# A decoder trunk layer on one core: the second gate's weight rows moved behind the first experts, a fifth ring slot, x loaded first

## The chip, the cores and the metric

The kernel runs on one core of a Trainium2 chip. The metric is the device time of one execution in microseconds; the time given for the kernel is the median of three executions.

## The reference, cut to what matters

One layer on 256 tokens of width 2048, all in float32. Everything with a weight is a matrix product; the modulation vectors come from one product of a single row.

```
mod = silu(c) @ w_ada + b_ada                 # one row, 2048 x 12288
sh1, sc1, g1, sh2, sc2, g2 = split(mod, 6)
h = rmsnorm(x, norm1_g) * (1 + sc1) + sh1
proj = h @ w_in                               # 2048 x 4928
o_a = HGRN2 recurrence on 4 x 1024 columns of proj, 8 heads
o_b = latent attention (q_a, kv_a, k_pe columns of proj), 8 heads, causal
x = x + g1 * (concat(o_a, o_b) @ w_out)       # 2048 x 2048
h2 = rmsnorm(x, norm2_g) * (1 + sc2) + sh2
y = MoE(h2): top-1 of 4 groups, top-2 of 8 experts in it; 32 SwiGLU experts,
    w_gate, w_up 2048 x 512, w_down 512 x 2048 each
x = x + g2 * y
```

## The kernel before, in words

**The weight ring.** All large weights are read once, as tiles `wch` of 128 x 4096 (2048 KB; some are smaller), by one queue, SP's, in the order of the list `items` (built from L104 on). A tile needs a free slot of the ring: RING = 4 slots at first, two more once the temporaries of the first part are closed (after `wout` 0, 1), and a seventh after the first part has ended. `ring_fill` (L165) issues the next load whenever `ring_done` (L183) frees a slot, so the list sets the order of the transfers and, with the text of the program, that of the work on each engine. A scheduler moves single instructions within that.

**The order of the list.** Two chunks of `ad1` (modulation columns for the first 512 columns of sh1 and sc1), `w_in` in quarters of the contraction (`wh` for halves of the first, `win` after) with twelve `adt` chunks merged in, the up-projections of q and kv, `w_out` in two halves of four chunks, and then 32 experts of four `gu` and two `dn` chunks. The other modulation chunks (`mods`: g1, a mixed block m2, g2 and at2) are set behind the items of `last` and the second half of `w_out` by the numbers in SPREAD.

**Two ways to compute the modulation.** An `ada` chunk holds 256 rows of w_ada by 2048 columns; `ada_chunk` multiplies it on TensorE with the silu(c) column as the stationary operand, L299 in the profile (`pada`, 8 matmuls in the program, 16 rows in the trace), and sums over eight chunks in one PSUM bank. `ada_end` copies the sum to `rows`, transposes it to columns (L312, `pcol`), or adds it to the row `brow` for g2. An `adt` or `at2` chunk holds transposed columns; `adt_chunk` multiplies it on VectorE by silu(c), broadcast over the partitions in `gate`, with a sum along the row: two passes of 128 x 2048 a chunk, L277 in the profile. at2 is the second half of sh2 and sc2.

**Projections.** `dense` (L413) splits each weight tile into a rounded part (ScalarE, L421) and the rest (VectorE, L422), and multiplies three products (L429 to L431 where the weights are stationary, L436 to L438 where the tokens are). Four split buffers lie between these engines. For `w_out`, `end` (L577) adds the gated result to x (L581). `hgrn` and `mla` (the attention) run in two halves between the chunks of `last`; each ends in transposes of its result (`pmt`, L567 and L844), which the output projection multiplies. `ptr` (L524) are the transposes at the head of an HGRN sweep, after a chain on VectorE and ScalarE.

**Routing and experts.** After `w_out` the router's result is computed in a chain of small instructions, and groups of four experts follow. For each, `dispatch` gathers the tokens' columns (L996), L1064 multiplies the `gu` chunks, `hidden` makes the SwiGLU product, `down` (L1037) multiplies the `dn` chunks (L1042), with the second gate multiplied into each piece of the result on VectorE (L1046), and `combine` (L1019) scatters the group's result back. `gate_rows` spreads g2 over the partitions after expert 0's `gu` chunks.

**The start.** `pc` (bias and gain columns), `pos_i`, one w_ada chunk, then x in four tiles, then the ring up to four chunks. `norm1` squares x (two tiles on ScalarE, two on VectorE), sums, takes the reciprocal root and multiplies x by it in eight pieces (L348). `make_h` then applies scale and shift (L391) and splits h.

Of the kernel before, what the change touches and what calls it, by code (L numbers as in the profile page):

```python
# [20 lines left out]
RING, NARENA, NTEMP, NSPLIT, RING2 = 4, 14, (8, 6), 4, 2  # L21

SPREAD = (1, 4, 7, 5, 5, 3, 1, 1, 1, 1, 1, 1, 0)
# [16 lines left out]
P_W = 154  # L40
# [4 lines left out]
def tile_hybrid_layer(ctx, tc, A, out):  # L45
# [44 lines left out]
    pos_i = cpool.tile([P, 2], I32, name="pos_i")  # L90
    nc.sync.dma_start(pc, A["pcol"])
    nc.sync.dma_start(pos_i, A["pos"])
# [14 lines left out]
    mods = [("ada", b, ch) for b in ("g1", "m2", "g2") for ch in range(8)] + [("at2", kt) for kt in range(8, 16)]  # L107
# [24 lines left out]
    items += experts  # L132
    index = {it: i for i, it in enumerate(items)}

    def source(it):
# [9 lines left out]
        if k == "ada":  # L145
            return A["w_ada"][("g1", "m2", "g2").index(it[1]), it[2]], 4096
        if k == "at2":
            return A["w_ada_t2"][it[1] - 8], 4096
# [16 lines left out]
    def ring_fill():  # L165
        while ring["next"] < ring["limit"]:
# [7 lines left out]
            nc.sync.dma_start(t[:, :cols], src)  # L174
# [13 lines left out]

    def log_exp_tables(inst):

        load = S.preload_act_table_set("natural_log_exp_and_others")
        tc.add_manual_dep(load.ins, inst.ins.name, mybir.DependencyInfo(mybir.DependencyClass.NoSync, mybir.DependencyReason.DATA),
                          reason="tables")
# [15 lines left out]
    crow = tmp([1, 1024], "crow"), tmp([1, 1024], "crow")  # L209
    for h in range(2):  # L210
        nc.scalar.dma_start(crow[h], A["crow"][:, 1024 * h:1024 * h + 1024])
# [5 lines left out]
    brow = big([P, 512], "brow")  # L217
    nc.scalar.dma_start(brow[0:128:32], A["b_g"])
# [10 lines left out]
    one_row = cpool.tile([1, P], F32, name="one_row")  # L229
    V.memset(one_row, 1.0)  # L230
    for h in range(4):
        ps = pm("pc")
        PE.matmul(ps, one_row, crow[h // 2][:, 512 * (h % 2):512 * (h % 2) + 512], start=True, stop=True)
        g = gate[:, 512 * h:512 * h + 512]
        i = S.activation(g, ps, AF.Sigmoid)
        if h == 3:
            log_exp_tables(i)
        V.tensor_mul(g, g, ps)

    acc = {}  # L240
    rows = cpool.tile([P, 512], F32, name="rows")
    sh1 = cpool.tile([P, 16], F32, name="sh1")
# [26 lines left out]
    def adt_chunk(it, sh, a, b, gain):  # L269

        w = ring_get(it)
        i = it[1]
# [31 lines left out]
    def ada_end(b):  # L304
        if b == "g2":
            for j in range(4):
                V.tensor_add(brow[32 * j:32 * j + 1], brow[32 * j:32 * j + 1], acc[b][32 * j:32 * j + 1])
            return
# [6 lines left out]
        if b == "g1":  # L315
            mod_shift(g1, t, P_BA + 64, 16)
        else:
            mod_shift(sh2[:, 0:8], t[:, 0:8], P_BA + 32, 8)
            mod_scale(a2[:, 0:8], t[:, 8:16], P_BA + 48, P_N2, 8)

    def norm1():

        sq = [big([P, 1024], "sq") for _ in range(4)]
        flat = [x.rearrange("p a b -> p (a b)") for x in xx]
        for j in range(4):
            if j < 2:
                S.activation(sq[j], flat[j], AF.Square)
            else:
                V.tensor_mul(sq[j], flat[j], flat[j])
        V.tensor_add(sq[0], sq[0], sq[1])  # L330
        V.tensor_add(sq[2], sq[2], sq[3])
        V.tensor_add(sq[0], sq[0], sq[2])
        V.tensor_add(sq[1][:, :512], sq[0][:, :512], sq[0][:, 512:])
        ps = pm("pss")
        for i in range(2):
            PE.matmul(ps[:, :256], ones, sq[1][:, 256 * i:256 * i + 256], start=i == 0, stop=i == 1)
# [894 lines left out]
```

## Time and profile before

| | us |
|---|---|
| median of three executions | 1521.19 (1522.1, 1519.09, 1521.19) |
| profiled execution | 1516.6 |
| its span, from the first instruction to the last | 1514.8 |
| TensorE busy | 1116.8 (74% of the span) |
| VectorE busy | 627.1 (41%) |
| ScalarE busy | 335.9 (22%) |
| read from HBM | 570.88 MB, 378 GB/s over the span |

The span lacks 1.8 us of the execution's time, which lie around it. TensorE's clock has two levels, 1.2 and 2.4 GHz; the profile gives the granted clock of a stretch as a share of the higher one, and it was 0.881 on the mean here. A stage of the program is a stretch of the span with the same kind of chunks; the bounds used below are 34.3 (first projection matmul), 232 (last pass of `w_in`'s third quarter), 433 (first matmul of the output projection), 556.3 (its end), 566.4 (all slots full), 579.9 (first slot free in the expert stage) and 1488.9 (last weights landed).

### The profile page before, as it was taken

How to read it: one execution, taken by the hardware profiler on the slowest of the kernel's cores; microseconds unless marked ns; L12 is line 12 of the kernel's file. 1: busy time of each engine (PE TensorE's matmuls, PEld its weight loads, DVE VectorE, ACT ScalarE, POOL GpSimd, SP SyncE). 2: the span in 40 equal slices, each digit the busy share in tenths (PEclk: the TensorE clock that was granted, in tenths of full speed). 3: DMA queues.
4: the chain of work that ended last, by engine and by line, in shares of the span. 5: the costliest groups of instructions: out<-in, count | busy, mean ns of one | idle time of the engine just before them, and what ended most of it. 6: DMA issues, size and time to landing. Idle time of an engine off the chain costs nothing.

```text
span 1514.8 us, 23373 instructions
## 1 busy us (share of the span) xinstructions
PE 1116.8 (74%) x10141; PEld 708.8 (47%) x10141; DVE 627.1 (41%) x1259; ACT 335.9 (22%) x679; POOL 5.2 (0%) x10
## 2 busy tenths in 40 slices
PE   5979999979888899666666566566667656666665
PEld 2867887637568796333323323323423423333222
DVE  6599998758778862220121122112102112112112
ACT  4734446536433343100100100100100100000000
POOL 0000000000000000000000000000000000000000
PEclk7999999999999998888889888878868889878677
DMA  8789796877979966999999999999999999999995
GB/s 351 270 330 356 300 356 248 333 282 300 373 306 390 389 261 275 427 428 426 427 428 426 427 427 428 426 428 426 427 428 427 427 427 427 427 427 427 427 427 230
DMA packets 42965, 574.52 MB, mean 379 GB/s; under 512 B 4838, under 2 KB 5094, under 8 KB 7660
## 3 DMA queue, kind: packets, MB, share of 16 engines
q1 hardware_dynamic: 41472, 570.51, 90.8%
q10 hardware_dynamic: 1388, 2.49, 0.4%
q8 instruction: 81, 1.33, 0.3%
q14 instruction: 24, 0.20, 0.0%
HBM read 570.88 MB, written 2.10 MB: 378 GB/s over the span
## 4 chain that ended last, share of the span: by engine, by line
DMA 48%; PE 37%; DVE 12%; ACT 2%; issue 1%; ACTq 0%; DVEq 0%
DMA wch<-in_w_gu_dram 37%; DMA wch<-in_w_down_dram 10%; PE pgu L1064 6%; PE pcmb L1019 3%; PE pacc L437 3%; PE pacc L438 3%; PE pacc L431 3%; PE pacc L429 3%; PE pacc L430 3%; DVE wch L277 3%; PE pacc L436 3%; PE py L1042 3%; DVE split L422 2%; PE pada L299 2%; PE pgat L996 1%; DVE proj L461 1%
## 5 line engine op out<-in xcount | busy, mean ns | idle before, releaser
L1064 PE MATMUL pgu<-wch,XT 128*32 128x256 f32 x4096 | 317.2, 464 | 201.3 <-DMA wch<-in_w_gu_dram 201.3
L1064 PEld LDWEIGHTS pgu<-wch,XT 128*32 128x32 f32 x4096 | 141.6, 128 | 368.1 <-DMA wch<-in_w_gu_dram 257.9
L1042 PE MATMUL py<-wch,hT 128*32 128x256 f32 x2048 | 163.2, 474 | 79.3 <-DMA wch<-in_w_down_dram 74.8
L1031 DVE TENSOR_TENSOR hid<-sgu,pgu 128x128 f32<-128x128 f32 x32 | 9.2, 288 | 476.3 <-ACT sgu L1029 476.3
L1046 DVE TENSOR_TENSOR Y<-py,gate 32x256 f32<-32x256 f32 x256 | 107.6, 420 | 213.8 <-PE py L1042 211.0
L421 ACT ACTIVATE split<-wch 128x512 fp32r<-128x512 f32 (+2 forms) x248 | 148.6, 614 | 186.5 <-PE pacc L431 81.4
L422 DVE TENSOR_TENSOR split<-wch,split 128x512 fp32r<-128x512 f32 (+2 forms) x248 | 158.4, 666 | 40.8 <-ACT split L421 38.5
L1042 PEld LDWEIGHTS py<-wch,hT 128*32 128x32 f32 x2048 | 77.8, 130 | 153.0 <-DMA wch<-in_w_down_dram 59.6
L1029 ACT ACTIVATE sgu<-pgu 128x128 f32<-128x128 f32 x32 | 8.9, 278 | 606.9 <-PE pgu L1064 606.9
L1001 ACT ACTIVATE XT<-pgat,sh,a 128x128 f32<-128x128 f32 x128 | 48.2, 457 | 224.9 <-PE pgat L996 224.9
L277 DVE SCALAR_TENSOR_TENSOR wch<-wch,gate 128x2048 f32<-128x2048 f32 x40 | 91.3, 2285 | 0.0
L429 PE MATMUL pacc<-mhi,split 128*128 128x256 f32 x256 | 74.2, 291 | 10.5 <-DVE xt L581 7.2
L437 PE MATMUL pacc<-split,hhi 128*128 128x512 f32 (+1 forms) x192 | 75.1, 391 | 5.9 <-DVE split L422 5.9
L431 PE MATMUL pacc<-mhi,split 128*128 128x256 f32 x256 | 73.5, 289 | 7.9 <-DVE split L422 7.9
L429 PE MATMUL pacc<-hhi,split 128*128 128x256 f32 x256 | 72.6, 287 | 7.7 <-ACT hhi L392 7.2
L436 PE MATMUL pacc<-split,hhi 128*128 128x512 f32 (+1 forms) x192 | 72.3, 389 | 3.0 <-ACT split L421 2.6
L430 PE MATMUL pacc<-hlo,split 128*128 128x256 f32 x256 | 73.1, 287 | 1.7 <-DVE hlo L393 1.7
L431 PE MATMUL pacc<-hhi,split 128*128 128x256 f32 x256 | 72.4, 287 | 2.3 <-DVE split L422 2.3
L430 PE MATMUL pacc<-mlo,split 128*128 128x256 f32 x256 | 73.8, 289 | 0.0
L438 PE MATMUL pacc<-split,hlo 128*128 128x512 f32 (+1 forms) x192 | 73.5, 385 | 0.0
L1019 PE MATMUL pcmb<-Y,pwt 128*128 128x512 f32 x128 | 59.2, 605 | 15.5 <-DVE Y L1046 15.5
L996 PEld LDWEIGHTS pgat<-ohr,x 128*128 128x128 f32 x512 | 63.8, 206 | 9.9 <-issue 9.0
(320 smaller groups left out, 1301.4 us busy)
## 6 DMA issues: line engine op xcount, KB each, us to landing
wch<-in_w_gu_dram SPq DMA_DIRECT2D x128, 2048.0 KB, 31.2
wch<-in_w_down_dram SPq DMA_DIRECT2D x64, 2048.0 KB, 31.8
wch<-in_w_ada_dram SPq DMA_DIRECT2D x28, 2048.0 KB, 10.0
wch<-in_w_ada_t_dram SPq DMA_DIRECT2D x20, 2048.0 KB, 9.8
wch<-in_w_in_dram SPq DMA_DIRECT2D x12, 2048.0 KB, 9.1
wch<-in_w_out_dram SPq DMA_DIRECT2D x8, 2048.0 KB, 14.0
wch<-in_w_in_h_dram SPq DMA_DIRECT2D x8, 1024.0 KB, 9.7
wch<-in_w_in_dram SPq DMA_DIRECT2D x3, 1664.0 KB, 6.7
```

What stands on the lines that cost most here:

```text
L277: V.scalar_tensor_tensor(wk, wk, 1.0, gate, op0=OP.mult, op1=OP.mult, accum_out=r[:, k:k + 1])
L421: S.activation(s[:, 0, :ncol], w, AF.Copy)
L422: V.tensor_sub(s[:, 1, :ncol], w, s[:, 0, :ncol])
L429: PE.matmul(o, s[:, 0, c], hi, start=first and h % 2 == 0, stop=False, skip_group_check=True)
L430: PE.matmul(o, s[:, 0, c], lo, start=False, stop=False, skip_group_check=True)
L431: PE.matmul(o, s[:, 1, c], hi, start=False, stop=stop, skip_group_check=True)
L436: PE.matmul(o, hi[:, c], s[:, 0, :ncol], start=first, stop=False)
L437: PE.matmul(o, hi[:, c], s[:, 1, :ncol], start=False, stop=False)
L438: PE.matmul(o, lo[:, c], s[:, 0, :ncol], start=False, stop=stop)
L1042: PE.matmul(py[32 * j:32 * j + 32, :256], H["T"][:, 32 * kt:32 * kt + 32], w[:, 1024 * kt + 256 * j:1024 * kt + 256 * j + 256], start=kt = ...
L1046: V.tensor_mul(Y[q][r:r + 32, 256 * j:256 * j + 256], py[32 * j:32 * j + 32, :256], gate[32 * j:32 * j + 32, c:c + 256])
L1064: PE.matmul(gu[32 * j:32 * j + 32, :256], XT[G4][kt // 8][:, kt % 8, 32 * e4:32 * e4 + 32], w[:, 1024 * i + 256 * j:1024 * i + 256 * j + 2 ...
```

## The change

- **The second gate behind the first experts.** The eight chunks for g2 leave `mods`; they are merged into `items`, one behind each of the six chunks of expert 1 and the first two of expert 2. `second_gate` multiplies such a chunk after its neighbour, and after the eighth calls `gate_rows`. The results of group 0 (experts 0 to 3) are therefore copied without the gate by ScalarE, in pieces of 32 x 256, and multiplied by it once per half after expert 3 on VectorE. g2's sum goes to `g2row`, and `gate_rows` adds the bias with a second matmul.
- **Second modulation all on TensorE.** The blocks m2 and at2 become sh2 and sc2, eight `ada` chunks each. With g1 that is 24 chunks before the experts on TensorE, as before, and none of them on VectorE but the twelve `adt`. The numbers of SPREAD put all of them ahead of `w_out`'s first half.
- **A fifth ring slot.** RING is 5, so the expert stage has 8 slots. Its memory comes from a smaller buffer for dynamic DMAs.
- **The start.** x is issued ahead of the first w_ada chunk, positions come inside `pc`, the rows of c and of the bias in one array. `norm1` squares three tiles on ScalarE and one on VectorE, and the multiplication of x by the reciprocal root moves to `make_h`, piece by piece.

```diff
-RING, NARENA, NTEMP, NSPLIT, RING2 = 4, 14, (8, 6), 4, 2
-SPREAD = (1, 4, 7, 5, 5, 3, 1, 1, 1, 1, 1, 1, 0)
+RING, NARENA, NTEMP, NSPLIT, RING2 = 5, 14, (8, 6), 4, 2
+SPREAD = (1, 4, 7, 6, 5, 0, 0, 0, 0, 0, 0, 0, 0)
...
-    mods = [("ada", b, ch) for b in ("g1", "m2", "g2") for ch in range(8)] + [("at2", kt) for kt in range(8, 16)]
+    mods = [("ada", b, ch) for b in ("g1", "sh2", "sc2") for ch in range(8)]
+    g2 = [("ada", "g2", ch) for ch in range(8)]
...
-    items += experts
+    items += experts[:6]
+    merge(experts[6:6 + 8], g2)
+    items += experts[6 + 8:]
...
-            nc.sync.dma_start(t[:, :cols], src)
+            load = nc.sync.dma_start(t[:, :cols], src)
+            if i == 0:
+                in_order(load, ring["behind"])
...
-        nc.sync.dma_start(xx[j], A["xT"][:, 4 * j:4 * j + 4])
-    ring["limit"] = 3
+        x_load = nc.sync.dma_start(xx[j], A["xT"][:, 4 * j:4 * j + 4])
+    ring["behind"] = x_load
+    ring["limit"] = 5
...
         if b == "g2":
-            for j in range(4):
-                V.tensor_add(brow[32 * j:32 * j + 1], brow[32 * j:32 * j + 1], acc[b][32 * j:32 * j + 1])
+            S.activation(g2row, acc[b], AF.Copy)
             return
...
-        for j in range(4):
-            for r in range(2):
-                v = xx[j][:, 2 * r:2 * r + 2]
-                V.tensor_mul(v, v, bc(y[:, None, :], [P, 2, 256]))
+        V.tensor_mul(rx, rx, t)
...
+        V.tensor_mul(xx[q][:, sl], xx[q][:, sl], bc(rx[:, None, :], [P, 2, 256]))
...
-        ("ada", "m2", 7): lambda: (router_weights(0), router_weights(1)),
-        ("at2", 11): lambda: router_weights(2),
-        ("at2", 15): lambda: router_weights(3),
+        ("ada", "sc2", 7): lambda: [router_weights(q) for q in range(4)],
...
-    def down(q, w, Y, r):
+    def down(q, w, Y, r, gated=True):
...
-            V.tensor_mul(Y[q][r:r + 32, 256 * j:256 * j + 256], py[32 * j:32 * j + 32, :256], gate[32 * j:32 * j + 32, c:c + 256])
+            if gated:
+                V.tensor_mul(Y[q][r:r + 32, 256 * j:256 * j + 256], py[32 * j:32 * j + 32, :256], gate[32 * j:32 * j + 32, c:c + 256])
+            else:
+                S.activation(Y[q][r:r + 32, 256 * j:256 * j + 256], py[32 * j:32 * j + 32, :256], AF.Copy)
...
+    def second_gate(it):
+
+        i = index[it] + 1
+        if items[i:] and items[i][0] == "ada":
+            ada_chunk(items[i][1], items[i][2])
+            if items[i][2] == 7:
+                gate_rows()
...
             ring_done(("gu", e, q))
+            second_gate(("gu", e, q))
...
-            down(q, ring_get(("dn", e, q)), Y4, 32 * e4)
+            down(q, ring_get(("dn", e, q)), Y4, 32 * e4, gated=G4 > 0)
             ring_done(("dn", e, q))
+            second_gate(("dn", e, q))
+            if e == 3:
+                V.tensor_mul(Y4[q], Y4[q], gate[:, 1024 * q:1024 * q + 1024])
...
-    nc = bacc.Bacc("TRN2", target_bir_lowering=False, num_devices=1)
+    nc = bacc.Bacc("TRN2", target_bir_lowering=False, num_devices=1, dynamic_dma_scratch_size=1024)
```

The order of the instructions moves at three places that the prediction speaks of. The numbers behind the names tell buffers apart; lines of the changed kernel are some six higher. The first is SP's queue at the start of the program. Before:

```order
L91 DMA pc<-in_pcol_dram 128x154
L92 DMA pos_i<-in_pos_dram 128x2
L174 DMA wch_99<-in_w_ada_dram 128x4096
L214 DMA x_91<-in_xT_dram 128x1024
L214 DMA x_92<-in_xT_dram 128x1024
L214 DMA x_93<-in_xT_dram 128x1024
L214 DMA x_94<-in_xT_dram 128x1024
L174 DMA wch_101<-in_w_ada_dram 128x4096
L174 DMA wch_103<-in_w_in_h_dram 128x2048
L219 DMA cst<-in_cst_dram 128x992
```

In the changed kernel:

```order
L91 DMA pc<-in_pcol_dram 128x156
L220 DMA x_87<-in_xT_dram 128x1024
L220 DMA x_88<-in_xT_dram 128x1024
L220 DMA x_89<-in_xT_dram 128x1024
L220 DMA x_90<-in_xT_dram 128x1024
L185 DMA wch_95<-in_w_ada_dram 128x4096
L185 DMA wch_97<-in_w_ada_dram 128x4096
L185 DMA wch_99<-in_w_in_h_dram 128x2048
L185 DMA wch_101<-in_w_ada_dram 128x4096
L185 DMA wch_103<-in_w_in_h_dram 128x2048
L224 DMA cst<-in_cst_dram 128x992
```

The four tiles of x now stand ahead of every chunk, and five chunks follow instead of four.

The second is PE ahead of the second HGRN sweep's transposes `ptr`, behind the dense rows of `w_in`'s last chunk. Before, with the mix transposes `pmt` of the attention's second half and the column transposes `pcol` between modulation rows:

```order
L299 MATMUL pada_3507<-wch_3482,ca 1x512 x8
L299 MATMUL pada_3507<-wch_3517,ca 1x512 x5
L844 MATMUL pmt_3334<-cst,o_3224 128x128 x4
L844 MATMUL pmt_3341<-cst,o_3224 128x128 x4
L312 MATMUL pcol_3485<-cst,rows 128x128 x4
L299 MATMUL pada_3507<-wch_3517,ca 1x512 x3
L299 MATMUL pada_3507<-wch_3527,ca 1x512 x8
L299 MATMUL pada_3507<-wch_3633,ca 1x512
L524 MATMUL ptr_3669<-cst,d_610_3647 128x128 x4
```

In the changed kernel the same `pmt` and `pcol` rows stand inside the dense rows, of which 21 more follow them; and then come three modulation chunks up to `ptr`:

```order
L437 MATMUL pacc_3564<-hhi_1661,split_3596 128x256
L850 MATMUL pmt_3333<-cst,o_3223 128x128 x4
L850 MATMUL pmt_3340<-cst,o_3223 128x128 x4
L316 MATMUL pcol_3484<-cst,rows 128x128 x4
L435 MATMUL pacc_3564<-hhi_1661,split_3596 128x256
```

```order
L436 MATMUL pacc_3565<-hlo_1662,split_3611 128x256
L437 MATMUL pacc_3565<-hhi_1661,split_3611 128x256
L304 MATMUL pada_3492<-wch_3481,ca 1x512 x8
L304 MATMUL pada_3492<-wch_3502,ca 1x512 x8
L304 MATMUL pada_3492<-wch_3512,ca 1x512 x8
L530 MATMUL ptr_3664<-cst,d_609_3642 128x128 x4
```

The `pmt` and `pcol` rows moved from behind that dense run into it.

The third is PE where the output projection begins, between the last `po` row of the second HGRN sweep and the mix transposes `pmt` of its result. Before, 15 modulation matmuls and 49 dense rows stand between them; the piece shows both ends:

```order
L555 MATMUL po_3731<-s_620_3695,b_3645 64x128
L299 MATMUL pada_3507<-wch_3633,ca 1x512 x7
L299 MATMUL pada_3507<-wch_3788,ca 1x512 x8
L429 MATMUL pacc_3832<-mhi_2501,split_3834 128x256
L430 MATMUL pacc_3832<-mlo_2502,split_3834 128x256
```

```order
L430 MATMUL pacc_3833<-mlo_2502,split_3879 128x256
L431 MATMUL pacc_3833<-mhi_2501,split_3879 128x256
L429 MATMUL pacc_3832<-mhi_3332,split_3894 128x256
L567 MATMUL pmt_3766<-cst,o_3720 128x128 x4
L567 MATMUL pmt_3773<-cst,o_3720 128x128 x4
```

In the changed kernel:

```order
L561 MATMUL po_3726<-s_619_3690,b_3640 64x128
L304 MATMUL pada_3492<-wch_3522,ca 1x512 x8
L304 MATMUL pada_3492<-wch_3628,ca 1x512 x8
L435 MATMUL pacc_3865<-mhi_2500,split_3867 128x256
L436 MATMUL pacc_3865<-mlo_2501,split_3867 128x256
L573 MATMUL pmt_3761<-cst,o_3715 128x128 x4
L573 MATMUL pmt_3768<-cst,o_3715 128x128 x4
L316 MATMUL pcol_3826<-cst,rows 128x128 x4
L437 MATMUL pacc_3865<-mhi_2500,split_3867 128x256
L435 MATMUL pacc_3865<-mhi_2500,split_3867 128x256
```

The mix transposes stand behind 16 modulation matmuls and two dense rows, and the column transposes of sc2 follow them.

## Rows read from the trace of the kernel before

**Rows 1.** The page's 40 slices: GB/s that the DMA engines moved in each.
```profile
GB/s 351 270 330 356 300 356 248 333 282 300 373 306 390 389 261 275 427 428 426 427 428 426 427 427 428 426 428 426 427 428 427 427 427 427 427 427 427 427 427 230
```

**Rows 2.** Windows by stage. Window, us; busy us of PE, PEld, DVE, ACT, POOL; PEclk, DMA share, GB/s.
```profile
60.00:232.00 172.00, 158.36 (x932) 134.92 (x931) 161.51 (x263) 80.53 (x140) 0.00 (x0) 0.99 0.87 334
232.00:433.00 201.00, 183.60 (x1247) 123.87 (x1245) 148.26 (x309) 104.36 (x207) 2.87 (x3) 0.97 0.75 298
433.00:556.30 123.30, 104.92 (x846) 102.11 (x843) 101.38 (x175) 42.30 (x67) 0.95 (x1) 0.93 0.89 365
566.40:579.90 13.50, 10.28 (x72) 8.81 (x72) 4.65 (x26) 4.30 (x12) 0.00 (x0) 0.62 0.00 1
579.90:1488.90 909.00, 592.98 (x6657) 298.79 (x6657) 162.94 (x370) 63.70 (x183) 0.00 (x0) 0.84 1.00 426
1488.90:1514.80 25.90, 14.93 (x113) 6.26 (x113) 9.18 (x17) 0.56 (x2) 0.00 (x0) 0.90 0.38 149
```

**Rows 3.** The chain of waits at its end: start us, us, engine, line.
```profile
1458.04 30.81 DMA wch<-in_w_gu_dram
1488.89 3.47 PE pgu L1064 x32
```

**Rows 4.** DMA issues by line: count, KB each, us from issue to landing.
```profile
wch<-in_w_gu_dram SPq DMA_DIRECT2D x128, 2048.0 KB, 31.2
wch<-in_w_ada_dram SPq DMA_DIRECT2D x28, 2048.0 KB, 10.0
```

**Rows 5.** Timeline of SP's queue at the expert stage's start: start us, us, operation.
```profile
579.94 8.02 SPq L174 DMA_DIRECT2D wch<-in_w_gu_dram  x3
```

**Rows 6.** Timeline of the start, all engines, and PE's wait before the first projection matmul.
```profile
9.78 0.33 SPq L174 DMA_DIRECT2D wch<-in_w_ada_dram  x1
13.76 1.22 DVE L329 TENSOR_TENSOR sq<-x 128x1024 f32<-128x1024 f32 x1 [0.99 <-DMA x<-in_xT_dram]
26.78 4.90 DVE L348 TENSOR_TENSOR x<-x,sq 128x512 f32<-128x512 f32 x8
...
PE pacc L429 <- ACT hhi L392: 7.0, 1, 7.0
```

**Rows 7.** DVE by line in the projection (60 to 232): busy us, mean ns, idle before.
```profile
L277 DVE SCALAR_TENSOR_TENSOR wch<-wch,gate 128x2048 f32<-128x2048 f32 x24 | 54.8, 2285 | 0.0
```

**Rows 8.** Attention (232 to 433): PE's longest wait, PE by line, PE's timeline.
```profile
PE ptr L524 <- DVE d L517: 9.0, 2, 5.7
L299 PE MATMUL pada<-wch,ca 128*1 128x512 f32 x352 | 49.1, 628 | 2.2 <-DVE sm L204 2.2
...
406.48 1.09 PE L844 MATMUL pmt<-cst,o 128*128 128x128 f32 x8
407.40 0.60 PE L312 MATMUL pcol<-cst,rows 128*128 128x128 f32 x4
```

**Rows 9.** Output projection (433 to 556): PE and DVE by line, PE's waits, timelines.
```profile
L629 PE MATMUL plog<-wr,xt 128*128 128x128 f32 x49 | 6.2, 277 | 0.0
L277 DVE SCALAR_TENSOR_TENSOR wch<-wch,gate 128x2048 f32<-128x2048 f32 x16 | 36.5, 2285 | 0.0
...
PE pacc L431 <- DVE split L422: 7.9, 2, 6.3
PE pacc L429 <- DVE xt L581: 7.2, 2, 5.6
PE pacc L429 <- ACT split L421: 3.2, 1, 3.2
...
429.46 3.61 PE L299 MATMUL pada<-wch,ca 128*1 128x512 f32 x30
433.33 0.27 PE L431 MATMUL pacc<-mhi,split 128*128 128x256 f32 x1
438.44 0.28 PE L429 MATMUL pacc<-mhi,split 128*128 128x256 f32 x1
437.73 1.22 DVE L561 TENSOR_TENSOR o<-o,proj 128x1024 f32<-128x1024 f32 x1
```

More of the change, by code (lines that the diff above doesn't have):

```diff
@@ L131, in tile_hybrid_layer, with in_order, log_exp_tables @@
     experts = [(k, e, q) for e in range(NE) for k, q in (("gu", 0), ("gu", 1), ("gu", 2), ("gu", 3), ("dn", 0), ("dn", 1))]
-    items += experts
+    items += experts[:6]
+    merge(experts[6:6 + 8], g2)
+    items += experts[6 + 8:]
     index = {it: i for i, it in enumerate(items)}
+    def in_order(inst, before):
+        tc.add_manual_dep(inst.ins, before.ins.name, mybir.DependencyInfo(mybir.DependencyClass.NoSync, mybir.DependencyReason.DATA),
+                          reason="order")
+    def log_exp_tables(inst):
+        load = S.preload_act_table_set("natural_log_exp_and_others")
+        in_order(load, inst)
+        return load
     def source(it):
@@ L145, in source @@
         if k == "ada":
[L146 to L148 removed]
+            return A["w_ada"][("g1", "sh2", "sc2", "g2").index(it[1]), it[2]], 4096
         if k == "win":
@@ L208, in tile_hybrid_layer @@
     gate = cpool.tile([P, D], F32, name="gate")
-    crow = tmp([1, 1024], "crow"), tmp([1, 1024], "crow")
-    for h in range(2):
-        nc.scalar.dma_start(crow[h], A["crow"][:, 1024 * h:1024 * h + 1024])
+    crow = big([P, 512], "crow")
+    nc.scalar.dma_start(crow[0:128:32], A["rows"][:, 0])
     xx = [tmp([P, 4, 256], "x") for _ in range(4)]
     for j in range(4):
-        nc.sync.dma_start(xx[j], A["xT"][:, 4 * j:4 * j + 4])
-    ring["limit"] = 3
+        x_load = nc.sync.dma_start(xx[j], A["xT"][:, 4 * j:4 * j + 4])
+    ring["behind"] = x_load
+    ring["limit"] = 5
     ring_fill()
-    brow = big([P, 512], "brow")
-    nc.scalar.dma_start(brow[0:128:32], A["b_g"])
     nc.sync.dma_start(cst, A["cst"])
@@ L228, in tile_hybrid_layer @@
     V.tensor_mul(ca, ca, cin)
-    one_row = cpool.tile([1, P], F32, name="one_row")
-    V.memset(one_row, 1.0)
     for h in range(4):
         ps = pm("pc")
-        PE.matmul(ps, one_row, crow[h // 2][:, 512 * (h % 2):512 * (h % 2) + 512], start=True, stop=True)
+        PE.matmul(ps, ones[32 * h:32 * h + 1, :], crow[32 * h:32 * h + 1], start=True, stop=True, tile_position=(32 * h, 0))
         g = gate[:, 512 * h:512 * h + 512]
@@ L236, in tile_hybrid_layer @@
         if h == 3:
-            log_exp_tables(i)
+            tables = log_exp_tables(i)
         V.tensor_mul(g, g, ps)
+    brow = cpool.tile([P, 512], F32, name="brow")
+    S.dma_start(brow[0:128:32], A["rows"][:, 1])
     acc = {}
     rows = cpool.tile([P, 512], F32, name="rows")
+    g2row = cpool.tile([P, 512], F32, name="g2row")
     sh1 = cpool.tile([P, 16], F32, name="sh1")
@@ L974, in gate_rows @@
             ps = pw("pg2")
-            PE.matmul(ps, ones[32 * j:32 * j + 1, :], brow[32 * j:32 * j + 1], start=True, stop=True, tile_position=(32 * j, 0))
+            for row in (g2row, brow):
+                PE.matmul(ps, ones[32 * j:32 * j + 1, :], row[32 * j:32 * j + 1], start=row is g2row, stop=row is brow,
+                          tile_position=(32 * j, 0))
             S.activation(gate[:, 512 * j:512 * j + 512], ps, AF.Copy)
```

73 lines of the change are left out of this document (32 added, 41 removed).

## The prediction

> **What bounds the kernel now.** I read the page's 40 slices first. In the last 24 slices but one the transfers run at 426 to 428 GB/s without a break; in the 16 before, the rate swings between 248 and 390 [rows 1]. So there are two kernels in one: an expert part that is as fast as its weights arrive, and a part before it that is not. The table by stage says the same in numbers [rows 2]: from 579.9 to 1488.9 the DMA share is 1.00 and PE is busy 593 of 909 us; from 60 to 433 the DMA share is 0.87 and 0.75, while PE is busy 158.4 of 172.0 us and 183.6 of 201.0. In the output projection (433.0 to 556.3) PE is busy 104.9 of 123.3 us and DVE 101.4. Between 566.4 and 579.9 the DMA moves nothing: all ring slots hold chunks that wait for the routing. The chain of waits confirms the expert part: it alternates between a chunk's transfer and the matmuls on it, up to the last landing at 1488.89 [rows 3]. After that 25.9 us remain, which the change doesn't touch.
>
> **What follows for any edit.** A chunk moved out of the first part into the expert part costs a whole transfer there and gives back only what it really held up before. The change does this with 8 chunks. All w_ada and expert chunks have the same 2048 KB [rows 4].
>
> **The change part by part**, against the profiled execution (1516.6 us, span 1514.8).
>
> *1. Eight chunks in the expert stage, one more ring slot: +34.3 us.* The first slot is released at 579.94 [rows 5], where seven slots are full. Of 192 expert chunks 7 are there already, so 185 land between 579.94 and 1488.85: 909 us / 185 = 4.91 us each. After the change 200 chunks follow the output projection's, and 8 slots hold the first 8 of them, so 192 land after the first release, 7 more: 7 x 4.91 = 34.4, of which I take 34.3. Were the eighth slot not filled in the idle stretch (13.5 us without transfers, and one chunk is 4.91, so it should be), it would be 8 x 4.91 = 39.3; that is the upper bound and 34.3 the lower. What the chunks make PE do is hidden: 8 chunks x 16 matmul rows at about 1.9 us a chunk (30 rows take 3.61 us [rows 9]) are 15 us, beside 909 - 593 = 316 us of PE idle. The two gate matmuls, group 0's copies on ACT (busy 63.7 of 909 us) and the two gate multiplies on DVE (162.9) lie in the same shade; without it the matmuls alone would cost their 15 us.
>
> The Trainium skill ("DMA: Bandwidth & Descriptors", section on where 436 GB/s comes from) holds that the HBM side binds such transfers at about 358 GB/s per core. By that figure a chunk would be an estimated 5.9 us and this term 41 us. The stage's own row has 426 GB/s with every engine busy, so here the measurement decides, and the sum goes by 4.91.
>
> *2. The start: -4.6 us.* The first projection matmul waits 7.0 us for a split of h [rows 6]. Back along that wait: the shift and scale stand on DVE behind eight x multiplies (from 26.78, 4.90 us, so 0.61 each), and these behind the squares of x, the first of which on DVE waits for x until 13.76. x was issued behind the first w_ada chunk. With x issued first, I let this chain start 3.4 us earlier (the first square follows a transfer of 2 MB now, x itself, in place of 2 MB and a quarter of x, and three squares go to ACT). Five multiplies instead of eight stand ahead of the shift: 3 x 0.61 = 1.8 us less. A memset between them is about 0.5 more. Sum -4.7, taken as -4.6. The second w_ada chunk, issued at 9.78 before [rows 6], is not held back longer, since the bytes ahead of it are the same. Bounds: 0 (the projection behind it runs at its own limit and takes the gain back) and -9 (w_ada's second chunk, too, comes early).
>
> *3. The projection, 60 to 232: -2 us.* DVE is busy 161.5 of 172.0 us [rows 2], 54.8 of them in the 24 passes of the modulation sum that stay on DVE [rows 7]. So the fifth slot can give only DVE's 10.5 us of idle time. I take a fifth of that, as the chunks arrive earlier; bounds 0 and -6.
>
> *4. Attention, 232 to 433: +1.2 us.* PE's largest wait there is 9.0 us in two parts for the decays of the HGRN heads [rows 8], a DVE chain, not a transfer. The order shows for the first of these sweeps more modulation matmuls ahead of its transposes than before, worth some 2.5 us of cover, and for the second that the mix and column transposes (1.09 and 0.60 us [rows 8]) moved in front of the last 21 dense rows, whose results start that DVE chain. They delay it by 1.7 us, and by an estimated 2 more where they wait for their own operand there: 3.7. Net +1.2. The 24 modulation chunks before the experts are as many PE rows as before (352 of them here, 49.1 us [rows 8]). Bounds: -10 (the extra slot removes over half of 17.4 us of PE idle) and +6 (both chains come late).
>
> *5. Output projection: -19.8 us.* This stage gets the gain. What leaves: eight chunks of DVE sums, 36.5 us of DVE work, and one modulation chunk on PE. The three waits of PE in this stage, 7.9, 7.2 and 3.2 us, are for a split or an x row update that stood behind such a 2.2-us sum on DVE [rows 9]; I let all 18.3 go. What stays for PE: 768 dense rows at 0.119 us (43 starts from 433.33 to 438.44: 5.11 us [rows 9]) are 91.3, router rows 6.2 and the mix transposes and small ones 1.4: 98.9 us. What comes: the transposes of the second modulation, 0.6; a wait at the entry, 3.0; the third x row, which now stands behind three chunk issues on SP, 1.0 (bounds 0 and 1.5). Together 103.5 against 123.3, so -19.8.
> The entry wait is this: before, 30 rows of modulation (3.61 us from 429.46) and 49 dense rows stood on PE between the last HGRN output and the mix transposes, whose operand's last multiply ran at 437.73 for 1.22 us [rows 9]. Now 32 modulation rows (3.9 us) and two dense rows stand there. The operand's chain took 9.4 us from 429.5 with four splits inside it; the order of DVE now has the splits behind it, about 3.5 us less but a memset more, so some 7 us against 4 us of cover: 3.0, between 2 (no memset in the way) and 5.5 (the chain as long as before). Bounds of the term: -23.6 (no wait at all) and -13 (a third of the splits still late).
>
> **Sum:** 34.3 - 4.6 - 2 + 1.2 - 19.8 = +9.1 us. From 1516.6 that is 1525.7 for an execution like the profiled one. That execution lies 4.6 us under the median of the three shown (1521.19), so the median to expect is 1530.3, said as **1530**. The bounds all at once give -14 and +28.
>
> **Rivals.** (a) *The fifth slot frees the middle.* PE idles 13.6 us in the projection and 17.4 in attention [rows 2]. If two thirds of these 31 us were chunks arriving late, 20.7 go in place of my net 0.8, and the sum is 9.1 + 0.8 - 20.7 = -10.8: 1510. For it: the DMA share of 0.75 in attention leaves room that a slot could use. Against: the long waits there name DVE [rows 8], and the projection's DVE has no room. It comes out on the faster side from about 12 us of the 31 on. Chance 0.20.
> (b) *The output projection does not shrink as said.* With DVE emptied, the splits wait for ACT and for the two split buffers PE holds, and with five w_out chunks in a row the x rows come late. If half of the 19.8 goes, the sum is +19: 1540. For it: DVE's splits already follow ACT in that stage. Chance 0.16.
> (c) *The front edits do nothing:* x ahead of w_ada and the slot move waits without shortening them. Terms 2 and 3 are 0: +15.7, 1537. For it: the projection after the start is at DVE's limit. Chance 0.12.
> (d) *It balances:* the start gives 9 us and the projection 6, so the sum is about +0.7: 1522. Chance 0.15.
> That HBM's figure of 358 GB/s from the skill's page should appear only now has no row for it; I give it no chance of its own.
>
> **How the numbers follow.** My forecast has 0.37. It, (b) and (c) are slower: 0.65. (d) is the same, 0.15; (a) is faster, 0.20. A difference of 0.2% is about 3 us, near what a measurement of this kernel can tell from none. The range runs from 1512, just above (a)'s figure, to 1540, (b)'s, which leaves out some 2 in 10: the deeper half of (a) and what lies over (b). My forecast's own range is 1525 to 1535.
>
> **What would show it.** In the profile of the changed kernel: the expert stage at 426 to 428 GB/s, some 943 us from the first release to the last landing (term 1); a tail of 25.9 us; the first projection matmul near 29.7 (term 2); some 398 us from that matmul to the first of the output projection, where there were 398.7 (terms 3 and 4); a wait of some 3 us ahead of the mix transposes, and an output projection of about 103 us without waits for splits over 3 us (term 5). I am wrong if the expert stage grows by less than 34 us, which would mean that transfers were not its limit, or if the part before the experts shortens by more than 34 us: then the slot or the start gave more than the waits show.

## The result, and the profile after

The changed kernel takes 1537.32 us (median of four, 1534.73 to 1539.75), the kernel before 1520.2 beside it: the ratio is 1.0111, 95% interval 1.009 to 1.0132. It is slower, by 17 us. The profiled execution took 1536.81 us with a span of 1534.6, 19.8 more than the span of before.

The page's slices for the changed kernel, share of the DMA engines in tenths and GB/s (answers to [rows 1]):

```profile
DMA  9798886887966459999999999999999999999995
GB/s 392 280 341 352 315 320 238 337 345 308 363 255 279 165 198 428 426 426 428 427 427 427 426 426 428 427 427 427 427 426 428 428 427 426 426 427 428 428 427 243
```

The saturated part begins one slice earlier and is longer; the two slices ahead of it have sunk to 165 and 198 GB/s. The windows by stage, with the bounds where the same events lie now (window, us; busy us of PE and PEld, which are TensorE's matmuls and weight loads, DVE, which is VectorE, ACT, which is ScalarE, and POOL; PEclk, the granted clock; DMA share, GB/s):

```profile
0.00:30.70 30.70, 12.82 (x53) 3.72 (x53) 17.64 (x39) 12.74 (x22) 1.30 (x6) 0.96 0.95 384
60.00:236.50 176.50, 160.82 (x933) 138.04 (x931) 164.29 (x267) 81.10 (x140) 0.00 (x0) 0.97 0.84 323
236.50:434.50 198.00, 180.08 (x1238) 120.42 (x1237) 146.32 (x310) 103.29 (x203) 3.81 (x4) 0.98 0.79 314
434.50:542.40 107.90, 101.83 (x830) 100.86 (x830) 62.34 (x111) 43.95 (x68) 0.00 (x0) 0.98 0.62 239
552.40:565.97 13.57, 10.21 (x82) 6.03 (x83) 5.35 (x30) 4.08 (x14) 0.00 (x0) 0.87 0.00 1
565.97:1509.54 943.57, 607.40 (x6789) 300.98 (x6789) 151.78 (x340) 78.22 (x220) 0.00 (x0) 0.85 1.00 426
1509.54:1534.60 25.06, 15.08 (x113) 6.24 (x113) 9.18 (x17) 0.56 (x2) 0.00 (x0) 0.84 0.39 156
```

Read against [rows 2]: the expert stage has grown from 909.0 to 943.6 us at the same 426 GB/s; the output projection has shrunk from 123.3 to 107.9, with DVE busy 62.3 us instead of 101.4, and its DMA share has fallen from 0.89 to 0.62. The stretch without transfers ahead of the experts is there as before, 13.57 us. So the change made room where the DMA engines had no use for it, and put its transfers where they had no time.

All runs by stage, each from one profiled execution; a stage ends where the next event begins. "Projection" runs from the first projection matmul to the last before attention's transposes, "routing" from the last matmul of the output projection to the first slot released by an expert chunk, "experts" from there to the first row of the last gu chunk. In e9, e10 and e12 dense rows of the output projection stand ahead of the second HGRN sweep, so their attention is shorter, and their output projection longer, than the same names mean in the other rows.

| run | first matmul | projection | attention | output proj. | routing | experts | tail | time (median) | ratio to before, 95% |
|---|---|---|---|---|---|---|---|---|---|
| before | 34.3 | 201.2 | 197.4 | 123.1 | 23.9 | 908.9 | 25.9 | 1520.2 | |
| changed | 30.7 | 205.8 | 198.1 | 107.9 | 23.6 | 943.6 | 25.1 | 1537.32 | 1.009 to 1.0132 |
| e1_g2_front | 30.5 | 205.8 | 197.9 | 118.2 | 31.4 | 904.2 | 29.2 | 1517.24 | 0.998 to 0.9999 |
| e2_four_slots | 30.3 | 203.5 | 206.0 | 103.9 | 25.2 | 948.6 | 26.4 | 1546.5 | 1.017 to 1.0204 |
| e3_x_second | 29.1 | 204.6 | 200.1 | 107.9 | 24.4 | 943.4 | 24.9 | 1536.82 | 1.0107 to 1.0141 |
| e4_before_five_slots | 34.4 | 200.8 | 193.3 | 125.1 | 24.9 | 905.2 | 25.8 | 1510.04 | 0.9928 to 0.9961 |
| e5_xt_other_queue | 31.0 | 205.8 | 197.9 | 101.2 | 23.6 | 943.5 | 25.0 | 1530.21 | 1.0054 to 1.0088 |
| e7_front_late_gate | 29.8 | 204.8 | 198.0 | 118.2 | 27.6 | 904.2 | 26.4 | 1512.82 | 0.995 to 0.9978 |
| e8_gap | 29.6 | 205.4 | 200.1 | 108.2 | 28.0 | 908.5 | 25.2 | 1507.32 | 0.9911 to 0.9945 |
| e9_before_gap | 34.2 | 199.7 | 173.9 | 126.4 | 28.5 | 906.7 | 28.5 | 1499.87 | 0.9846 to 0.989 |
| e10_gap_xt | 34.3 | 202.3 | 174.2 | 123.0 | 23.5 | 911.1 | 25.8 | 1496.0 | 0.9831 to 0.9869 |
| e11_x_late | 35.9 | 196.0 | 198.0 | 107.9 | 24.3 | 943.3 | 25.2 | 1534.95 | 1.0087 to 1.0121 |
| e12_gap_all | 34.4 | 200.7 | 174.1 | 122.7 | 22.9 | 911.7 | 25.8 | 1494.46 | 0.9818 to 0.9853 |

How far a stage repeats shows in five of these rows: up to the end of attention the changed kernel, e1, e5, e7 and e8 have the same instructions in the same order on TensorE, VectorE and ScalarE. Their first matmul comes at 29.6 to 31.0, the projection takes 204.8 to 205.8 us and attention 197.9 to 200.1. A difference of 2 us in one stage of one execution can be chance.

### The profile page after: what moved, and what is told of

Its sections match the earlier page's. It is cut to its first block, busy times and chain, and to the rows that moved or that the text cites. A ratio compares the mean times of both kernels' runs of the same rounds, so it can differ in the third digit from the quotient of the medians.

```text
span 1534.6 us, 23595 instructions
## 1 busy us (share of the span) xinstructions
PE 1127.1 (73%) x10281; PEld 708.7 (46%) x10281; DVE 576.3 (38%) x1170; ACT 350.4 (23%) x714; POOL 5.1 (0%) x10
## 5 line engine op out<-in xcount | busy, mean ns | idle before, releaser
L1079 PE MATMUL pgu<-wch,XT 128*32 128x256 f32 x4096 | 304.0, 449 | 206.9 <-DMA wch<-in_w_gu_dram 204.0
L1079 PEld LDWEIGHTS pgu<-wch,XT 128*32 128x32 f32 x4096 | 138.2, 125 | 365.0 <-DMA wch<-in_w_gu_dram 257.1
L1046 PE MATMUL py<-wch,hT 128*32 128x256 f32 x2048 | 167.8, 484 | 81.1 <-DMA wch<-in_w_down_dram 77.7
L1051 DVE TENSOR_TENSOR Y<-py,gate 32x256 f32<-32x256 f32 x224 | 94.2, 420 | 193.5 <-PE py L1046 191.1
L304 PE MATMUL pada<-wch,ca 128*1 128x512 f32 x512 | 70.7, 633 | 10.1 <-DMA wch<-in_w_ada_dram 8.6
L1023 PE MATMUL pcmb<-Y,pwt 128*128 128x512 f32 x128 | 63.4, 641 | 19.4 <-DVE Y L1051 13.6
## 6 DMA issues: line engine op xcount, KB each, us to landing
wch<-in_w_gu_dram SPq DMA_DIRECT2D x128, 2048.0 KB, 36.1
```

The costliest lines, as they stand in the source:

```text
L304: PE.matmul(acc[b][32 * j:32 * j + 1, :], ca[:, kt:kt + 1], w[:, o:o + 512], start=kt == 0, stop=kt == 15)
L1046: PE.matmul(py[32 * j:32 * j + 32, :256], H["T"][:, 32 * kt:32 * kt + 32], w[:, 1024 * kt + 256 * j:1024 * kt + 256 * j + 256], start=kt = ...
L1051: V.tensor_mul(Y[q][r:r + 32, 256 * j:256 * j + 256], py[32 * j:32 * j + 32, :256], gate[32 * j:32 * j + 32, c:c + 256])
L1079: PE.matmul(gu[32 * j:32 * j + 32, :256], XT[G4][kt // 8][:, kt % 8, 32 * e4:32 * e4 + 32], w[:, 1024 * i + 256 * j:1024 * i + 256 * j + 2 ...
```

## The experiments

### Eight chunks back ahead of the experts: e1 and e7

```diff
-    items += experts[:6]
-    merge(experts[6:6 + 8], g2)
-    items += experts[6 + 8:]
+    items += experts
...
-SPREAD = (1, 4, 7, 6, 5, 0, 0, 0, 0, 0, 0, 0, 0)
+SPREAD = (1, 4, 7, 6, 5, 1, 1, 1, 1, 1, 1, 1, 1)
```

> The changed kernel with the eight g2 chunks back ahead of the experts, all on TensorE, one behind each of the eight w_out chunks; the gate is multiplied in each piece again. Theory A (a chunk behind the experts costs a whole transfer, a chunk ahead of them only its TensorE rows): 184 chunks land after the first release instead of 192, so the expert stage falls from 943.5 to about 904 us; the output projection grows by 8 x 1.87 = 15 us, from 108 to 123; time 1537 - 39 + 15 = 1513. Rival B (the front part is held by something that the chunks lengthen by as much, slots or splits): expert stage 904, but the part ahead of it grows by 30 us or more, time 1528 or more.

The time was 1517.24 us, 20 less than the changed kernel. The expert stage measured 904.2 us as said:

```profile
583.67:1487.90 904.23, 600.78 (x6657) 301.26 (x6657) 162.88 (x370) 64.08 (x184) 0.00 (x0) 0.83 1.00 426
```

With 184 landings that is 4.914 us a chunk; the changed kernel's 943.57 / 192 is 4.914 as well, and before's 908.9 / 185 is 4.913. The price of a chunk in that stage is the same in these three. The output projection grew by 10.3 us, less than the 15 of theory A, because seven of the eight chunks lie in it and because two waits for x rows (4.6 us, shown under e5 below) are gone with them. Against e5, which has no such waits either, the seven chunks cost 17.0 us, 2.4 each, more than the 1.87 of A. The routing grew by 7.8 us, which A did not have. PE's timeline in e1's routing (start us, us, engine, line):

```profile
556.58 3.29 PE L301 MATMUL pada<-wch,ca 128*1 128x512 f32 x16
559.80 3.96 PE L663 MATMUL px<-cst,xt 128*128 128x128 f32 x32
563.69 1.33 PE L975 MATMUL pg<-g2row,ones 1*128 1x512 f32 x4
564.65 1.23 PE L975 MATMUL pg<-brow,ones 1*128 1x512 f32 x4
...
569.27 2.07 PE L975 MATMUL pg<-g2row,ones 1*128 1x512 f32 x2
571.13 1.91 PE L975 MATMUL pg<-brow,ones 1*128 1x512 f32 x2
...
573.27 2.07 PE L975 MATMUL pg<-g2row,ones 1*128 1x512 f32 x2
```

The gate rows (pg) and one modulation chunk stand between the routing's own rows. e7 takes the gate rows out: group 0 stays ungated as in the changed kernel, and `gate_rows` is called at expert 1. Against e1:

```diff
-        if e == 0:
+        if e == 1:
             gate_rows()
...
-            down(q, ring_get(("dn", e, q)), Y4, 32 * e4, gated=True)
+            down(q, ring_get(("dn", e, q)), Y4, 32 * e4, gated=G4 > 0)
```

> As e1 (g2's chunks ahead of the experts, one behind each w_out chunk), with group 0 ungated as in the changed kernel and the gate rows only at expert 1. Theory A (e1's routing chain was 29.4 us, 7.8 more than in the changed kernel, since the gate rows and one modulation chunk stand in it on TensorE): the chain falls by the gate rows' share, 4 to 7 us, time 1517 - 5 = 1512. Rival B (the chain is VectorE's and the gate rows only filled TensorE's idle time): chain 29, time 1517.

The routing fell from 31.4 to 27.6 us, 3.8 where theory A said 4 to 7, and the time to 1512.82. The same eight chunks, ahead of the experts instead of behind the first of them, are worth 24.5 us (1537.32 to 1512.82).

### The fifth slot: e2 and e4

```diff
-RING, NARENA, NTEMP, NSPLIT, RING2 = 5, 14, (8, 6), 4, 2
+RING, NARENA, NTEMP, NSPLIT, RING2 = 4, 14, (8, 6), 4, 2
```

> The changed kernel with RING = 4, so 7 slots in the expert stage; all else as changed. Theory A (the fifth slot is worth one preloaded chunk and nothing else): the expert stage grows by 4.9 us to 948.4, the part ahead of it stays within 2 us, time 1542. Rival B (the slot also frees TensorE in the projection and attention): the part ahead grows by 6 us or more, time 1548 or more. Rival C (the slot costs something early, by earlier transfers beside other work): the part ahead shrinks by 3 us or more, time 1539 or less.

Time 1546.5, between A and B. The expert stage is 948.6 us, 5.0 more, as one chunk should be; the part ahead of it is 2.9 us longer (releases start at 568.87 instead of 565.97). Within that part the slot does more: attention is 7.9 us longer without it, the output projection 4.0 shorter. The projection does not get longer without it.

```diff
-RING, NARENA, NTEMP, NSPLIT, RING2 = 4, 14, (8, 6), 4, 2
+RING, NARENA, NTEMP, NSPLIT, RING2 = 5, 14, (8, 6), 4, 2
...
-    nc = bacc.Bacc("TRN2", target_bir_lowering=False, num_devices=1)
+    nc = bacc.Bacc("TRN2", target_bir_lowering=False, num_devices=1, dynamic_dma_scratch_size=1024)
```

> The kernel before with RING = 5 and the smaller buffer for dynamic DMAs, and nothing else. Theory A (one preloaded chunk): expert stage 909 - 4.9 = 904 us, the part ahead of it within 2 us of 579.9, time 1515. Rival B (the slot frees the middle): the part ahead 6 us or more shorter, time 1509 or less. Rival C (it is slower ahead of the experts): time 1519 or more.

On the kernel before, the slot alone gives 1510.04 us, ratio 0.9945, some 9 us. The profiled executions show 3.7 us of it in the expert stage and 4.1 in attention, with 2.0 given back in the output projection. The difference of the medians is larger than that of the two spans (5.3); the span of before is that of an execution faster than its median. So the slot paid; e7, which is the whole change but for the place of g2's chunks, is at 1512.82 no faster than the slot alone.

In attention the slot came with another order on PE: between the mix transposes and the `ptr` rows of the first HGRN sweep, before and e2 (four slots) have 16 modulation rows, e4 and the changed kernel (five slots) 48. PE's idle time in that stage fell from 17.4 us to 13.7 in e4. Its wait for `ptr`, 9.0 us before [rows 8], fell to 5.3, two waits for splits (2.0 us) went, and one for the mix transposes came. PE's waits in attention of e4, and below them of the changed kernel:

```profile
PE ptr L524 <- DVE d L517: 5.3, 2, 3.4
PE pmt L844 <- DVE o L838: 1.8, 1, 1.8
```

```profile
PE ptr L530 <- DVE d L523: 6.3, 2, 4.4
PE pmt L850 <- DVE o L844: 2.6, 2, 1.8
```

None of PE's waits in that stage names a transfer, before or in e4. So rival (a) of the prediction held for attention in small, but the reason it gave, chunks that arrive late, does not show; how much the order alone is worth was not tried. For the projection it did not hold.

### Where x stands at the start: e3 and e11

```diff
+    ring["limit"] = 1
+    ring_fill()
     xx = [tmp([P, 4, 256], "x") for _ in range(4)]
...
-            if i == 0:
-                in_order(load, ring["behind"])
```

> The changed kernel with the first w_ada chunk issued ahead of x again; all else as changed. Theory A (the projection is at VectorE's limit and takes back what the start gives): the first projection matmul comes 2 to 4 us later than at 30.7, the first matmul of the output projection within 1.5 us of 434.5, time within 2 us of 1537. Rival B (the start's gain goes through): both 2 to 4 us later, time 1540.

The first matmul came at 29.1, earlier than with x first (30.7), against both theories, though hardly outside the 29.6 to 31.0 at which that start repeats; the time was 1536.82, the same. e11 issues x behind three chunks (limit 3 in the same place).

> The changed kernel with x issued behind the first three chunks (two of w_ada, one of w_in) instead of ahead of them. The start is made worse on purpose, to see whether the projection takes that back too. Theory A (the projection's end is set by VectorE's order from the first adt pass on, which waits little for the start): the first projection matmul moves from 30.7 to 35 or later, the end of the projection (236.5) by less than half of that, time within 3 us of 1537. Rival B (the start is on the path and its gain was lost elsewhere): the whole delay of 4 us or more reaches the expert stage, time 1541 or more.

PE's timeline at the first projection matmul, in the changed kernel and then in e11, where the modulation rows ahead of it are shown too:

```profile
30.70 0.58 PE L435 MATMUL pacc<-hhi,split 128*128 128x256 f32 x1 [5.61 <-ACT hhi L398]
```

```profile
31.19 3.22 PE L263 MATMUL pad<-wch,ca 128*1 128x512 f32 x16
35.87 0.51 PE L435 MATMUL pacc<-hhi,split 128*128 128x256 f32 x2 [1.46 <-ACT hhi L398]
```

The first matmul came 5.2 us later, yet the projection ended at 231.9 instead of 236.5, and the time was 1534.95, 2.4 us less. Rival B is out: no such delay reaches the end. The test is milder than 5.2 us, though. The chunk of modulation rows at 31.19 stands behind the first 36 dense matmuls in the changed kernel, so PE had done more before it began, and the 100th dense matmul came only 1.2 us later (51.1 against 49.9). The order on VectorE moved as well, so e11 shows that a later x need cost nothing, and not what a later start costs with all else in place.

Between before and the changed kernel the lead can be followed on PE by counting dense matmuls. The 200th starts at 72.9 us before and at 69.7 after, a lead of 3.2; the 300th at 94.1 and 94.3, none. Between these two VectorE is busy nearly all the time in both (first row: before; second: the changed kernel):

```profile
72.90:94.10 21.20, 17.97 (x101) 14.60 (x100) 21.02 (x34) 7.31 (x13) 0.00 (x0) 1.00 0.89 333
69.70:94.30 24.60, 20.10 (x101) 16.66 (x100) 23.32 (x38) 8.36 (x15) 0.00 (x0) 0.86 0.93 341
```

The windows that follow, of the changed kernel, show the same limit:

```profile
80.00:100.00 20.00, 15.71 (x72) 12.54 (x72) 18.84 (x32) 6.28 (x12) 0.00 (x0) 0.84 0.92 347
100.00:120.00 20.00, 17.39 (x91) 14.33 (x92) 19.68 (x33) 8.54 (x14) 0.00 (x0) 0.92 0.91 339
120.00:140.00 20.00, 19.02 (x129) 17.26 (x128) 19.84 (x33) 9.86 (x16) 0.00 (x0) 1.00 0.91 366
140.00:160.00 20.00, 18.35 (x103) 15.52 (x102) 19.83 (x34) 8.98 (x15) 0.00 (x0) 1.00 0.79 307
```

From 80 us on DVE is busy 18.8 to 19.8 of every 20 us. Its own first adt pass came at 66.5 us before and at 65.8 after, a lead of 0.7 us where the start had 3.6.

The projection ends anywhere between 231.9 and 236.8 in these kernels. One piece of that goes with the order of DVE's instructions: from the 800th to the 900th dense matmul the five kernels with the changed kernel's order take 18.6 to 18.7 us, the other eight 16.0 to 17.3. The changed kernel is 1.6 us ahead of before at the 800th and 0.9 behind at the 900th. The rest was not tried apart; among the five with the same order the later starts go with the later ends.

### The waits in the output projection: e5

PE's waits there in the changed kernel (engine, line waited for: us in total, times, longest), and the DVE rows at the first of them:

```profile
PE pacc L435 <- DVE xt L587: 4.6, 2, 2.3
PE pmt L573 <- DVE o L567: 1.4, 1, 1.4
PE pacc L435 <- ACT split L427: 1.2, 1, 1.2
```

```profile
460.26 0.69 DVE L428 TENSOR_TENSOR split<-wch,split 128x512 fp32r<-128x512 f32 x1 [0.75 <-ACT split L427]
461.70 0.69 DVE L428 TENSOR_TENSOR split<-wch,split 128x512 fp32r<-128x512 f32 x1 [0.74 <-ACT split L427]
462.30 1.66 DVE L587 SCALAR_TENSOR_TENSOR xt<-pacc,g,xt 128x256 f32<-128x256 f32 x4
```

The x update (L587) frees the accumulators that PE wants next, and stands behind a split for a later chunk, which waits for ScalarE, and that for PE. DVE had idle time; the order held the update back. The order had it there because the load of xt stands behind five w_out chunks on SP's queue.

```diff
-            nc.sync.dma_start(xt[j], A["xT"][:, 4 * j:4 * j + 4])
+            S.dma_start(xt[j], A["xT"][:, 4 * j:4 * j + 4])
```

> The changed kernel with the four x rows of the output projection (xt) issued on ScalarE's queue instead of SP's, so they don't stand behind five w_out chunks; the scheduler then places the xt updates on VectorE about 14 rows earlier. Theory A (the two waits of 2.3 us for xt in the output projection come from where the updates stand in VectorE's order, and that from the SP queue): both waits are gone, the projection falls from 107.9 to about 103 us, time 1537 - 4.6 = 1533. Rival B (TensorE then waits for the splits behind the updates instead): the projection stays within 1.5 us, time 1536 to 1539.

The output projection fell to 101.2 us and the time to 1530.21. PE's remaining waits in that stage of e5, and its window:

```profile
PE pmt L573 <- DVE o L567: 1.4, 1, 1.4
PE pacc L435 <- ACT split L427: 1.2, 1, 1.2
```

```profile
434.69:535.94 101.25, 99.87 (x830) 99.26 (x830) 62.22 (x111) 43.89 (x68) 0.00 (x0) 1.00 0.65 254
```

Theory A, with some 2 us more than its two waits. These lie in PE's busy time: the same 830 rows take 99.87 us instead of 101.83, at a granted clock of 1.00 instead of 0.98. The clock was not moved by itself in any run.

### Chunks in the gap ahead of the experts: e8, e9, e10 and e12

The 13.6 us without transfers come from slots full of expert chunks that nobody can use yet. Modulation chunks can be used there. e8 is e7 with xt on the other queue and five of g2's chunks behind the last w_out chunk:

```diff
-SPREAD = (1, 4, 7, 6, 5, 1, 1, 1, 1, 1, 1, 1, 1)
+SPREAD = (1, 4, 7, 6, 5, 0, 1, 0, 1, 0, 1, 0, 5)
```

> As e7, with three of g2's chunks in the output projection and five behind it, multiplied on TensorE during the routing chain, and xt on ScalarE's queue. Theory A (13.6 us without transfers ahead of the experts are lost because all slots hold expert chunks; chunks that are used up in the chain let the transfers go on): no stretch without transfers from 545 us on, first expert matmul near 571, last weights 189 x 4.91 = 928 us after about 549, time 1505. Rival B (the five chunks delay the routing on TensorE by their whole 9.4 us or more and nothing is won): time 1512 or more.

Time 1507.32, nearer to A. The transfers no longer stop (first row: e8's routing; second: the changed kernel's, both from the last matmul of the output projection on), and the five chunks take PE 10.46 us in it:

```profile
543.37:571.34 27.97, 26.60 (x223) 17.04 (x222) 10.59 (x53) 10.11 (x27) 0.00 (x0) 0.88 0.97 395
```

```profile
542.40:565.97 23.57, 19.73 (x153) 15.26 (x152) 10.19 (x53) 9.81 (x26) 0.00 (x0) 0.86 0.35 134
```

```profile
547.61 10.46 PE L301 MATMUL pada<-wch,ca 128*1 128x512 f32 x80
```

The routing is 4.4 us longer than in the changed kernel, less than half of that. Against e7, which has one chunk there already, four chunks moved: the output projection is 10.0 us shorter (118.2 to 108.2), the routing 0.4 longer and the expert stage 4.3 longer, because the preloaded chunks were still on their way when the first slot came free (DMA share 0.98 in the last 5.3 us ahead of it, 0.00 in e7). So the gap does not give back its whole 13.6 us; the move is worth 5.5 (1512.82 to 1507.32). xt's other queue has no visible part in it, since PE's waits in e7's output projection are already e5's two (1.4 and 1.2 us); a run without it was not made. e9 does the same on the kernel before with five slots (e4): at2 stays on VectorE, and four g2 chunks move into the gap.

```diff
-SPREAD = (1, 4, 7, 5, 5, 3, 1, 1, 1, 1, 1, 1, 0)
+SPREAD = (1, 4, 7, 4, 3, 2, 1, 1, 1, 1, 1, 1, 4)
...
-    mods = [("ada", b, ch) for b in ("g1", "m2", "g2") for ch in range(8)] + [("at2", kt) for kt in range(8, 16)]
+    mods = [("ada", b, ch) for b in ("g1", "m2", "g2") for ch in range(8)]
+    mods[20:20] = [("at2", kt) for kt in range(8, 16)]
```

> The kernel before with five slots (e4), and four of g2's chunks behind the output projection, multiplied during the routing chain; at2 stays on VectorE. Theory A: three modulation chunks less in attention are 5.6 us, and the transfers no longer stop ahead of the experts, which is worth up to 13.5 us less 2 to 4 for the chunks in the chain: 1510 - 16 = 1494. Rival B (the chain grows by the four chunks' 7.5 us and the slots run dry at the experts' start): time 1505 or more.

1499.87 us, 10 less than e4, and not for A's reasons alone. The last matmul of the output projection comes at 534.1 instead of 553.6. Four chunks fewer on PE are 7.5 us of that. The order also put dense rows of the output projection ahead of the second HGRN sweep's transposes, whose wait on PE fell from 5.3 us to 1.7. The rest was not taken apart. PE's longest waits in e9's output projection:

```profile
PE pacc L430 <- DVE xt L582: 10.6, 2, 8.9
PE pacc L430 <- ACT split L422: 3.9, 1, 3.9
```

e10 adds e5's change to e9, and e12 adds to that the ungated group 0 and the gate rows at expert 1, as in e7.

> As e9 (the kernel before with five slots and four g2 chunks in the routing chain), with xt on ScalarE's queue. Theory A (e9's 10.6 us of TensorE's wait for xt in the output projection come from the place of the updates behind the SP queue, as in the changed kernel): 5 to 10 us of it go, time 1500 - 7 = 1493. Rival B (in e9 the updates stand behind the at2 passes on VectorE, whatever the queue): within 2 us of 1500.

> As e10, with group 0 ungated and the gate rows at expert 1, as in the changed kernel but with g2's sum taken from the bias row. Theory A (of the gate rows some 2.6 us stand in the routing chain on TensorE): the first expert matmul 1 to 3 us earlier than in e10, time as much less. Rival B (they fill idle time there): within 1 us of e10.

e10 took 1496.0 us: the wait for xt is gone, but 6.9 us for splits came in its place, so 4 us remain of the 7 (A in its mechanism, not its size). e12 took 1494.46, its first expert matmul at 552.90 instead of 555.24. That looks like A, but 1.7 of these 2.3 us are there at the last matmul of the output projection (531.95 instead of 533.69), ahead of the routing, where the two kernels differ, and the routing itself is only 0.6 us shorter; among the changed kernel, e3, e5 and e11, whose routing is the same, it differs by 0.8. Between A and B e12 does not decide. It has the lowest median here, 0.9836 of the kernel before (0.9818 to 0.9853), though not clear of e10's (0.9831 to 0.9869).

## Why the prediction was right, and where its steps were wrong

The direction and the range held: 1537.3 against a forecast of 1530 in 1512 to 1540. The forecast's own, narrower range, 1525 to 1535, did not, and the sum of the terms came to twice what was said. The term that carries the direction was right in mechanism and in size; that the time still fell inside the range is in part luck, since the two spans differ by 19.8 us and the medians by 17: the spans' 19.8 on the 1521.19 that the forecast started from would have been 1541, outside. Of the bounds given for all terms at once, -14 and +28, the upper one should be +32, with the 39.3 of term 1. Step by step, from the two profiled executions:

- **Term 1, the experts, said +34.3: measured +34.6.** The reason held in every run: 4.91 to 4.92 us a chunk, with 184, 185, 192 or 193 of them, in the nine kernels whose preloaded chunks had all landed before the stage, and the same 427 GB/s in the four where some had not (e8, e9, e10 and e12). The matmuls, gate rows and copies put beside it cost nothing that shows.
- **Term 2, the start, said -4.6: measured -3.6, and worth nothing.** The step that failed is the one behind it: I took the first matmul to be on the path. The count of dense matmuls shows PE's lead gone at the 300th, and e11 that a later x need cost nothing. I had named the way (the projection at its limit takes the gain back) as a bound only, and as rival (c).
- **Term 3, the projection, said -2: measured +4.6.** The slot gives nothing there (e2: 203.5 without it, 205.8 with it). With term 2 the sum is +1.0 where -6.6 stood; this is the larger miss, and in these two terms rival (c) came true. That the time is (c)'s figure, 1537, is in part luck: (c) has neither the miss of term 5 (4.6 us) nor the 2.8 us by which the medians differ less than the spans, and these partly offset each other. For the slot (c) did not hold: the slot paid in attention and in the expert stage.
- **Term 4, attention, said +1.2: measured +0.7,** near by luck, from other parts. Of the two HGRN waits the first fell from 3.3 to 1.9 us where 2.5 us of cover were said, and the second from 5.7 to 4.4 where 3.7 more was said, so the delay of that sweep did not come. Against these 2.7 us stand one more modulation chunk (368 rows instead of 352) and a new wait of 2.6 us for the mix transposes. e4 and e2 put the slot, with the order that came with it, at 4 to 8 us here.
- **Term 5, the output projection, said -19.8: measured -15.2.** That the waits behind the DVE sums go was right. The entry's 3.0 came out at 2.6 (1.4 for the mix transposes and, just ahead of the stage's first matmul, 1.2 for a split). The xt term was mis-sized: 1.0 was said for a late third row, 4.6 measured, at two updates that the order of DVE held back. PE's rows, said as 99.5 us (98.9 and 0.6), kept it busy for 101.8. e5 removes both waits and reaches 101.2, below my 103.5. Rival (b) named this mechanism; it took a quarter of the term, not half.
- **Routing and tail:** 0.3 and 0.8 us less. The sum is +20, where +9.1 was said; the spans differ by 19.8, the medians by 17.

The trace does not agree with the 358 GB/s of the Trainium skill ("DMA: Bandwidth & Descriptors", "Where 436 GB/s comes from") that the prediction weighed: the stage moved 426 GB/s again.

## What to carry to other kernels

Ask of each stage what ends it, and move work only out of the stage's own limit: a weight chunk used in a transfer-bound stage cost its whole transfer (4.91 us here), however much idle time the engines had, while in the output projection ahead of it a chunk cost 2.4 us (e1 against e5), and in the stretch where transfers stood still about half of that (e8 against e7: 0.4 and 4.3 us for four). An earlier start is worth something only if no saturated engine lies between it and the end; a run with a later start tells whether one does, if the order behind the start stays the same. When an engine with idle time makes another wait, look at what stands ahead of the late instruction in its fixed order, and which load put it there.

## What the runs showed of the hardware

The transfer rate of the expert stage did not move with anything tried: 426 to 427 GB/s in all thirteen kernels, with seven or eight slots in the ring, although a gu chunk's time from issue to landing (median) rose from 31.2 us before to 36.1 in the changed kernel with its eighth slot, and is 31.1 in e2 with seven. What I had not expected is that the modulation matmuls in the routing run at little more than half their pace in e1, 16 rows in 3.29 us, where 30 rows took 3.61 us in the kernel before [rows 9]. The granted clock of that stretch of e1 is 0.55, near the lower of the two levels; in the 4.28 us ahead of it, in which PE was busy throughout, it was 1.00. What made it fall was not tried.

```profile
552.30:556.58 4.28, 4.28 (x40) 4.20 (x39) 1.71 (x5) 1.20 (x3) 0.00 (x0) 1.00 0.62 264
556.58:559.80 3.22, 3.22 (x18) 0.44 (x17) 2.27 (x15) 0.41 (x2) 0.00 (x0) 0.55 0.02 5
```
